# Loading one row block of the last batch in three parts: 1632 columns on all 128 partitions, 544 columns as 36 and 92 partitions

## The chip, the cores and the metric

The kernel runs on one core of a Trainium2 chip. The metric is the device time of one execution in microseconds (us), as the median of several runs. Engines are named as in the profile: PE (TensorE, matrix products and transposes), PEld (its weight loads), DVE (VectorE), ACT (ScalarE), POOL (GpSimd) and SP (SyncE). Sixteen DMA engines move data between the chip's main memory and the core's on-chip memory of 128 partitions.

## The reference

There are eight pairs of matrices of 2176 by 2176 float32 values. For each pair the trace of the product is wanted, so eight numbers in all:

```python
B, N = 8, 2176
prod = np.matmul(a, b)
traces = np.diagonal(prod, axis1=1, axis2=2).sum(axis=-1)   # shape (8,)
```

The trace needs no full product: it is the sum over all i and k of a[i, k] * b[k, i]. Each element of `a` and of `b` is used once, against the transposed partner.

## The kernel before

**Tiling.** N is 17 blocks of P = 128. The kernel speaks of 17 "rows" of `b`: row v is the block of 128 matrix rows from 128 v on, one matrix row on each partition and 2176 columns along it. For each batch the matrix `a` is loaded, transposed by the PE in 128 by 128 squares (lines 151 and 175), and copied out of PSUM by ACT and DVE into the tile `at` (lines 121 and 123). Then `b` is loaded, and `multiply_reduce` (line 128, on DVE) multiplies rows of `at` by rows of `b` and sums along the columns into one column of partial sums.

**Loads.** All loads but the first go out from POOL by `dma_start`, and convert float32 in main memory to bfloat16 in the destination. `in_order` ties each issue behind the issue before it, so POOL issues them in the order in which they are written. `fetch` (line 75) is the ordinary load: all 128 partitions, one contiguous stretch for each partition.

**The last batch** is cut finer, because nothing follows that could cover its end. `a` comes as two groups of six rows and one of five, and `b` by `fine = [4, 4, 4, 2, 1, 1, 1]` rows to a load. In this order:

- rows 0-3, 4-7 and 8-11: three loads of four rows. DVE multiplies rows 0-3, 4-7 and 8-10; row 11 goes to PE.
- rows 12 and 13: one load, all on PE.
- row 14: one load, then one DVE instruction over 2176 columns.
- row 15 (`SHARED_ROW`): one load; PE takes columns 0 to 1023 and DVE the other 1152.
- row 16: three loads by `LAST_PIECES` (line 273): columns 768-2175, then 256-767, then 0-255. DVE multiplies columns 768-1407 (640 of them), PE takes the rest.

A row on PE is 17 products of 128 by 128 (line 287) that add into the one PSUM tile `trace_ps`. Products into `unread` stand between them; nothing reads their result. At the end DVE multiplies `trace_ps` by the identity and sums it (tile `diagonal`, line 128), PE adds up the partitions (line 306), DVE adds up the columns (line 309), and SP stores the eight numbers (line 312).

**Semaphores of the loads.** The loads from POOL take eight completion semaphores in turn. A load that takes a semaphore again waits for the load that had it eight loads earlier, if nothing before has made that sure. Of the last loads, the piece of 256 columns waits in this way for the load of rows 0-3.

Of the kernel before, what the change touches and what calls it, by code (L numbers as in the profile page):

```python
# [10 lines left out]
def row_groups(p, rows):  # L11

    groups, at = [], 0
    for m in rows:
        groups.append((at, m))
        at += m * p
    return groups
# [3 lines left out]
def kernel(  # L21
# [6 lines left out]
    nc = tc.nc  # L28
    P = 128
    BATCH, N, N2 = a.shape  # L30
# [21 lines left out]

    LAST_PIECES = [(6 * P, 11 * P, N), (2 * P, 2 * P, 6 * P), (0, 0, 2 * P)]

    KEEP_BUSY = {11: 7, 13: 6, SHARED_ROW: 2}

    const = ctx.enter_context(tc.tile_pool(name="const", bufs=1))
# [7 lines left out]
    loaded = []  # L65

    def in_order():

        return tc.issue_after(loaded[-1].ins) if loaded else nullcontext()

    def fetch(t, src, start, g, m):

        rows = src[start:start + P * g * m, :].rearrange("(g p r) k -> p g (r k)", g=g, r=m)
        with in_order():
            issued = nc.gpsimd.dma_start(out=t.rearrange("p (g r) k -> p g (r k)", g=g), in_=rows)  # L75
        loaded.append(issued)
        return t

    def load(src, start, g, m):

        if g * m <= MID:
            t = middle.tile([P, MID, N], bf16, tag="middle")
        else:
            t = stage.tile([P, MOST, N], bf16, tag="stage")
        return fetch(t[:, 0:g * m, :], src, start, g, m)

    def load_first(src, start):

        words = stage.tile([P, MOST, N], bf16, tag="stage")
        plain = words.bitcast(f32).rearrange("p r k -> p (r k)")[:, :N]  # L90
        half = N // 2
        t = single.tile([P, 1, N], bf16, tag="single")
        nc.sync.dma_start(out=plain, in_=src[start:start + P, :])
        nc.scalar.copy(out=t[:, 0, :half], in_=plain[:, :half])  # L94
        nc.vector.tensor_copy(out=t[:, 0, half:], in_=plain[:, half:])  # L95
        return t
# [4 lines left out]
    def constants():  # L101
        identity32 = const.tile([P, P], f32, tag="identity32")
        make_identity(nc, identity32)
        identity16 = const.tile([P, P], bf16, tag="identity16")
        make_identity(nc, identity16)
        ones = const.tile([P, 1], f32, tag="ones")
        nc.vector.memset(ones, 1.0)
        sums = const.tile([P, (BATCH - 1) * per_batch], f32, tag="sums")
        late = const.tile([P, 2 * NT], f32, tag="late")
        diagonal = const.tile([P, P], bf16, tag="diagonal")  # L110
        result = const.tile([P, BATCH], f32, tag="result")
        tiles.update(ones=ones, sums=sums, late=late, result=result, diagonal=diagonal)
        tiles[f32], tiles[bf16] = identity32, identity16
# [12 lines left out]
    def multiply_reduce(x, y, acc, out=None):  # L126

        nc.vector.tensor_tensor_reduce(  # L128
            out=x if out is None else out, in0=x, in1=y, scale=1.0, scalar=0.0,
            op0=MUL, op1=ADD, accum_out=acc,  # L130
        )
# [54 lines left out]
    def multiply_on_pe(at, row, v, lo, hi):  # L186

        for c in range(lo, hi, P):
            pe_work.append((at[:, v, c:c + P], row[:, c:c + P]))

    def keep_pe_busy(at, v):

        x = at[:, v, :]
        pe_work.extend([(x[:, 0:P], x[:, 0:4 * P])] * KEEP_BUSY.get(v, 0))

    late = []
    ahead = None
    for bi in range(BATCH):
        last = bi == BATCH - 1
        b_groups = row_groups(P, fine if last else even)  # L200


        at = at_pool.tile([P, NT, N], bf16, tag="at")
        at_row = 0
        for g, m in last_loads if last else a_loads if bi else first_loads:
            start = at_row * P
            at_row += g * m
            if not tiles:
                a_t = load_first(a[bi], start)
                ahead = load(a[bi], start + P * m, *first_loads[1])  # L210
                with tc.issue_after(loaded[-1].ins):
                    constants()
            elif ahead is not None:
                a_t, ahead = ahead, None
            else:
                a_t = load(a[bi], start, g, m)
            for s in range(g):
                last_transpose = transpose_group(
                    at, a_t[:, s * m:(s + 1) * m, :], start + s * m * P, m, b_groups
                )  # L220


        copies_end = last_copy
        acc = tiles["late"] if last else tiles["sums"][:, bi * per_batch:(bi + 1) * per_batch]
        cols = 0

        def on_dve(v0, rows):

            nonlocal cols
            m = rows.shape[1]  # L230
            with tc.issue_after(copies_end.ins):
                multiply_reduce(
                    at[:, v0:v0 + m, :].rearrange("q v x -> q (v x)"),
                    rows.rearrange("q v x -> q (v x)"),
                    acc[:, cols:cols + 1],
                )
            cols += 1

        if not last:
            at_row = 0  # L240
            for g, m in b_loads:
                on_dve(at_row, load(b[bi], at_row * P, g, m))
                at_row += g * m
            continue

        used = MOST
        for start, m in b_groups:
            v0 = start // P
            if start < N - P:

                if used + m > MOST:
                    shared = stage.tile([P, MOST, N], bf16, tag="stage")
                    used = 0
                b_t = fetch(shared[:, used:used + m, :], b[bi], start, 1, m)
                used += m
                if v0 == SHARED_ROW:
                    row = b_t[:, 0, :]
                    multiply_on_pe(at, row, v0, 0, HALF)
                    keep_pe_busy(at, v0)
                    late.append((at[:, v0, HALF:], row[:, HALF:]))  # L260
                    continue
                mine = [s for s in range(m) if v0 + s not in PE_ROWS]
                if mine:
                    on_dve(v0 + mine[0], b_t[:, mine[0]:mine[-1] + 1, :])
                for s in range(m):
                    if s not in mine:
                        multiply_on_pe(at, b_t[:, s, :], v0 + s, 0, N)
                        keep_pe_busy(at, v0 + s)
                continue
            row = shared[:, used, :]  # L270
            for lo, mid, hi in LAST_PIECES:
                with in_order():
                    loaded.append(nc.gpsimd.dma_start(  # L273
                        out=row[:, lo:hi], in_=b[bi, start:start + P, lo:hi]
                    ))
                multiply_on_pe(at, row, v0, mid, hi)
                if mid > lo:
                    late.append((at[:, v0, lo:mid], row[:, lo:mid]))
# [5 lines left out]
    for n, (x, y) in enumerate(pe_work):  # L284
        real = y.shape[-1] == P
        with tc.issue_after(before.ins):
            before = nc.tensor.matmul(  # L287
                trace_ps if real else unread[:, 0:4, :], x, y,
                start=(n == 0 or not real), stop=(n == len(pe_work) - 1 or not real),
# [7 lines left out]
        out=result[:1, 0:done],  # L297
        in_=total[:, 0:early].rearrange("o (b n) -> o b n", n=per_batch),
        axis=mybir.AxisListType.X,
    )  # L300
    for x, y in late:
# [8 lines left out]
        out=result[:1, done:BATCH], in_=total[:, early:early + cols], axis=mybir.AxisListType.X  # L310
    )
    nc.sync.dma_start(
        out=out.rearrange("(a b) -> a b", a=1),
        in_=tiles["result"][:1, :BATCH],
# [31 lines left out]
```

## Time and profile before

| what | value |
|---|---|
| median of 3 runs | 708.98 us (708.90 to 709.16) |
| span of the profiled execution | 707.1 us |
| own time of the profiled execution | not recorded; the median is 1.88 us above the span |
| moved by DMA (as bytes written) | 152.31 MB, 215 GB/s on the mean |
| DMA packets | 7698 |
| busy share of the span | PE 28%, DVE 55%, ACT 29%, POOL 3% |
| read from main memory | 303.04 MB, 429 GB/s over the span |
| loads of the last batch's `b`, issue to landing, median | 33.1 us for each of rows 14 and 15; 33.4 us for the 256-column piece |

A busy time is the sum of an engine's instructions. The DMA line of the profile gives, for each of 40 equal slices of the span, the mean busy share of the 16 DMA engines in tenths; in a window's row the same is given as a fraction. "Issue to landing" is the time from the DMA's issue on POOL to its last completion. The times in the text are counted from the span's start.

### The profile page before, as it was taken

The page shows a single profiled execution, that of the slowest core. Times are in us where ns is not written, and L with a number is a line of the kernel's source. Part 1 is how long each engine was busy: PE and PEld are TensorE (multiplying, and loading weights), DVE is VectorE, ACT ScalarE, POOL GpSimd, SP SyncE. Part 2 cuts the span into 40 slices and gives each one's busy share as a digit, 9 for nine tenths or more (in the row PEclk, how much of TensorE's full clock was granted, in tenths as well). Part 3 has the DMA queues.
Part 4 walks back from the last instruction along what each step waited for, and adds up shares of the span by engine and source line. Part 5 has one row for each costly group of instructions (what it writes and reads, how often), then busy time and mean ns, then how long its engine had stood idle before and what let it go on. Part 6 is the DMA issues. An engine that isn't in the chain of part 4 may idle for free.

```text
span 707.1 us, 3653 instructions
## 1 busy us (share of the span) xinstructions
PE 200.8 (28%) x1569; PEld 179.8 (25%) x1569; DVE 386.8 (55%) x98; ACT 202.9 (29%) x160; POOL 24.7 (3%) x47
## 2 busy tenths in 40 slices
PE   2235003450134501344012440134301353003806
PEld 1234002440123401243012430124301343003703
DVE  0105488154881539616397163961629627395497
ACT  2327002470024700346004350044500445002910
POOL 1000000000000000000000000000000000000100
PEclk9759555695557955678556785567755677555957
DMA  9999999999999999999999999999999999999997
GB/s 236 213 217 212 225 206 214 216 224 214 224 215 213 223 213 214 216 223 218 215 217 216 215 222 213 216 223 211 221 216 216 222 214 217 216 220 213 217 211 151
DMA packets 7698, 152.31 MB, mean 215 GB/s; under 512 B 642, under 2 KB 898, under 8 KB 1282
## 3 DMA queue, kind: packets, MB, share of 16 engines
q0 software_dynamic: 7536, 150.96, 99.6%
q1 hardware_dynamic: 146, 1.11, 0.4%
q8 instruction: 12, 0.20, 0.1%
q14 instruction: 4, 0.03, 0.0%
HBM read 303.04 MB, written 0.00 MB: 429 GB/s over the span
## 4 chain that ended last, share of the span: by engine, by line
DVE 33%; another core or an unknown queue 27%; ACT 13%; PE 12%; DMA 11%; issue 3%; POOL 0%; ACTq 0%; DVEq 0%; POOLq 0%
DVE at L128 33%; ACT at L123 13%; PE ps L151 9%; DMA t<-in_a_dram 6%; DMA shared<-in_b_dram 5%; PE ps L175 2%; DVE at L121 0%; POOL shared L75 0%; PE trace_ps L287 0%; POOL shared L273 0%; POOL identity masks.py:199 0%; POOL identity masks.py:197 0%; ACTq L123 0%; DVE diagonal L128 0%
## 5 line engine op out<-in xcount | busy, mean ns | idle before, releaser
L123 ACT COPY at<-ps 128x1536 bf16<-128x1536 bf16 (+5 forms) x158 | 200.5, 1359 | 467.2 <-DVE sums L128 308.6
L128 DVE CUSTOM_DVE_ANT_0 at<-at,t 128x10880 bf16<-128x10880 bf16 (+1 forms) x14 | 272.0, 19426 | 96.3 <-DMA t<-in_b_dram 86.6
L151 PE MATMUL ps<-identity,t 128*128 128x128 f32 x833 | 147.1, 344 | 471.6 <-DMA t<-in_a_dram 378.6
L151 PEld LDWEIGHTS ps<-identity,t 128*128 128x128 f32 x833 | 131.3, 209 | 484.6 <-issue 380.3
L121 DVE COPY at<-ps 128x1536 bf16<-128x1536 bf16 (+3 forms) x52 | 83.4, 1604 | 205.8 <-PE ps L151 152.5
L175 PE MATMUL ps<-identity,t 128*128 128x128 bf16 x646 | 45.8, 227 | 11.0 <-ACT at L123 8.6
L175 PEld LDWEIGHTS <-t 128*128 128x128 bf16 x646 | 43.1, 119 | 14.7 <-issue 14.2
L128 DVE CUSTOM_DVE_ANT_0 at<-at,shared 128x8704 bf16<-128x8704 bf16 (+4 forms) x6 | 29.9, 5001 | 1.8 <-DMA shared<-in_b_dram 1.7
L75 POOL DMA_DIRECT2D t<-in_a_dram x16 | 10.1, 637 | 294.1 <-DVE sums L128 267.4
L75 POOL DMA_DIRECT2D t<-in_b_dram x14 | 8.7, 628 | 290.8 <-PE ps L175 290.5
L287 PEld LDWEIGHTS <-at 128*128 128x128 bf16 x86 | 6.8, 112 | 24.7 <-issue 23.9
L287 PE MATMUL trace_ps<-shared,at 128*128 128x128 bf16 x71 | 5.8, 241 | 21.0 <-DMA shared<-in_b_dram 20.9
L75 POOL DMA_DIRECT2D shared<-in_b_dram x6 | 3.2, 541 | 59.3 <-DVE sums L128 38.9
L287 PE MATMUL unread<-at 128*128 128x512 bf16 x15 | 5.2, 496 | 0.0
L296 DVE TENSOR_REDUCE result<-total 1x7 f32<-1x14 f32 x1 | 0.2, 159 | 7.8 <-PE total L295 7.8
L95 DVE CAST t<-words 128x1088 bf16<-128x1088 f32 x1 | 0.7, 727 | 4.9 <-DMA words<-in_a_dram 4.9
L94 ACT CAST t<-words 128x1088 bf16<-128x1088 f32 x1 | 1.1, 1099 | 3.7 <-DMA words<-in_a_dram 3.7
L273 POOL DMA_DIRECT2D shared<-in_b_dram x3 | 1.6, 552 | 1.9 <-DMA shared<-in_b_dram 1.9
L94 ACT ACT_TABLE_LOAD x1 | 1.3, 1283 | 0.7 <-PEq L330 0.7
L128 DVE DVE_READ_ACCUMULATOR2_ANT sums<- 128x1 f32 x14 | 1.2, 83 | 0.0
L128 DVE CUSTOM_DVE_ANT_0 diagonal<-identity,trace_ps 128x128 bf16<-128x128 f32 x1 | 0.3, 289 | 0.6 <-PE trace_ps L287 0.6
L128 DVE DVE_READ_ACCUMULATOR2_ANT late<- 128x1 f32 x7 | 0.6, 83 | 0.0
(12 smaller groups left out, 2.1 us busy)
## 6 DMA issues: line engine op xcount, KB each, us to landing
t<-in_a_dram POOLq DMA_DIRECT2D x8, 6528.0 KB, 55.1
t<-in_b_dram POOLq DMA_DIRECT2D x7, 6528.0 KB, 52.8
t<-in_b_dram POOLq DMA_DIRECT2D x7, 2720.0 KB, 22.1
t<-in_a_dram POOLq DMA_DIRECT2D x7, 2720.0 KB, 24.8
shared<-in_b_dram POOLq DMA_DIRECT2D x3, 2176.0 KB, 36.0
t<-in_a_dram POOLq DMA_DIRECT2D x1, 2176.0 KB, 14.7
words<-in_a_dram SPq DMA_DIRECT2D x1, 1088.0 KB, 5.0
shared<-in_b_dram POOLq DMA_DIRECT2D x1, 1088.0 KB, 30.5
```

The costliest lines, as they stand in the source:

```text
L75: issued = nc.gpsimd.dma_start(out=t.rearrange("p (g r) k -> p g (r k)", g=g), in_=rows)
L94: nc.scalar.copy(out=t[:, 0, :half], in_=plain[:, :half])
L95: nc.vector.tensor_copy(out=t[:, 0, half:], in_=plain[:, half:])
L121: last_copy = nc.vector.tensor_copy(out=dst, in_=src)
L123: nc.scalar.copy(out=dst, in_=src)
L128: nc.vector.tensor_tensor_reduce(out=x if out is None else out, in0=x, in1=y, scale=1.0, scalar=0.0, op0=MUL, op1=ADD, accum_out=acc,)
L151: nc.tensor.transpose(ps[:, n * m + r, :], words[:, r, c0:c0 + step * (P - 1) + 1:step], tiles[f32],)
L175: last_transpose = nc.tensor.transpose(ps16[:, n, r, :], a_t[:, r, c0:c0 + step * (P - 1) + 1:step], tiles[bf16],)
L273: loaded.append(nc.gpsimd.dma_start(out=row[:, lo:hi], in_=b[bi, start:start + P, lo:hi]))
L287: before = nc.tensor.matmul(trace_ps if real else unread[:, 0:4, :], x, y, start=(n == 0 or not real), stop=(n == len(pe_work) - 1 or not ...
L296: nc.vector.reduce_sum(out=result[:1, 0:done], in_=total[:, 0:early].rearrange("o (b n) -> o b n", n=per_batch), axis=mybir.AxisListType.X,)
```

## The change

Row 14 of the last batch is loaded by the new function `fetch_uneven` in place of `fetch`. It sees each matrix row of 2176 columns as two halves of 1088 and issues three loads in place of one:

- columns 272 to 1087 of both halves (1632 columns together), on all 128 partitions;
- columns 0 to 271 of both halves (544 columns together), on the first 36 partitions;
- the same 544 columns, on the other 92 partitions.

The bytes, the destination, and the work on them are as before; DVE's product over row 14 now needs all three loads.

```diff
+    UNEVEN_ROW, UNEVEN, LOW_SHARE = 14, 272, 36
...
+    def fetch_uneven(t, src, start):
+
+        halves = t[:, 0, :].rearrange("p (h k) -> p h k", h=2)
+        rows = src[start:start + P, :].rearrange("p (h k) -> p h k", h=2)
+        for p0, p1, lo, hi in [
+            (0, P, UNEVEN, N // 2), (0, LOW_SHARE, 0, UNEVEN), (LOW_SHARE, P, 0, UNEVEN)
+        ]:
+            with in_order():
+                loaded.append(nc.gpsimd.dma_start(
+                    out=halves[p0:p1, :, lo:hi], in_=rows[p0:p1, :, lo:hi]
+                ))
+        return t
...
-                b_t = fetch(shared[:, used:used + m, :], b[bi], start, 1, m)
+                if v0 == UNEVEN_ROW:
+                    b_t = fetch_uneven(shared[:, used:used + m, :], b[bi], start)
+                else:
+                    b_t = fetch(shared[:, used:used + m, :], b[bi], start, 1, m)
```

With two more loads in the list, the eight completion semaphores fall differently on the loads that follow. In the built program row 15's load now waits for the last load of `a`, the 1408-column piece for the load of rows 0-3, the 512-column piece for rows 4-7, and the 256-column piece for rows 8-11.

## The prediction

> **What bounds the kernel now.** I read the page's slices first: the DMA row is at 9 tenths in 39 of 40 slices and 7 in the last, while no compute engine is near full. Then the chain that ended last, from 640 us on: its last long link is the load of `b`.
>
> ```profile
> 668.07 35.47 DMA shared<-in_b_dram
> 703.54 0.04 issue
> 703.58 0.63 PE trace_ps L287 x6
> 704.21 0.03 issue
> ```
>
> So the end is: last load lands, PE's last products (L287), the diagonal, the sum, the store. Whatever moves the last landing moves the end one for one. Next, windows over the last microseconds. Columns: window, length, busy time and count for PE, PEld, DVE, ACT and POOL, granted PE clock, DMA share, GB/s.
>
> ```profile
> 700.00:701.00 1.00, 0.00 (x0) 0.00 (x0) 1.00 (x1) 0.00 (x0) 0.00 (x0) 1.00 1.04 192
> 701.00:702.00 1.00, 0.78 (x10) 0.64 (x10) 0.94 (x3) 0.00 (x0) 0.00 (x0) 1.00 0.91 153
> 702.00:703.00 1.00, 0.32 (x3) 0.05 (x1) 0.65 (x3) 0.00 (x0) 0.00 (x0) 1.00 0.45 71
> 703.00:704.00 1.00, 0.86 (x12) 0.66 (x11) 0.76 (x2) 0.00 (x0) 0.00 (x0) 1.00 0.15 20
> ```
>
> The reader sees all 16 DMA engines busy until 701, then a ragged end: 0.45 of them in the next-to-last and 0.15 in the last microsecond with transfers. The time is set by the latest engines, not by the mean. The sixteen completions of the 256-column load say how ragged: eight come at 701.53 to 702.38, four at 702.76 to 702.88, four at 703.68 to 703.89. Their mean is 702.58, so even a perfect levelling could bring 703.89 - 702.58 = 1.31 us.
>
> Where the three groups come from is in the queue rows:
>
> ```profile
> q0 software_dynamic: 7536, 150.96, 99.6%
> q8 instruction: 12, 0.20, 0.1%
> ```
>
> The packet records show 12 instruction packets of 16384 bytes, 0.89 to 1.00 us each. Following each engine's sequence of packets by start and duration, all run at one rate, and after an instruction packet one engine is about 0.9 us behind for good. Eight engines are never hit, four once, four twice. The records carry no engine numbers.
>
> **The change, part by part.** Packets of one size follow each other in the records at fixed distances: 4352 bytes (row 14's now) 323 ns, 2816 bytes 210 ns, 1024 bytes 79 ns, 512 bytes 41 ns; each load ends with a completion packet of 21 ns. Interpolated, an estimate from these rows: 1632 bytes (816 columns) 123.5 ns, 544 bytes (272 columns) 43.4 ns.
>
> Removed, on each engine: 8 rows x 323 + 21 = 2605 ns.
> Added, first load: 8 rows x 2 x 123.5 + 21 = 1997 ns on each engine.
> Added, the other two: how 36 or 92 partitions are shared among 16 engines no row shows; every load of the trace from POOL has 128. Bounds: as even as the row of 128 (8 pieces-of-row per engine), or packed in equal whole shares on few engines. The sizes speak for the second: 36 = 12 x 3 and 92 = 4 x 23, and 12 + 4 = 16. I take that. Twelve engines then carry 3 x 2 x 43.4 + 21 = 281 ns and a bare completion packet of 21; four carry 23 x 2 x 43.4 + 21 = 2017 ns and 21.
>
> Sums: twelve engines 1997 + 281 + 21 = 2299, against 2605: **0.31 us earlier**. Four engines 1997 + 2017 + 21 = 4035: **1.43 us later**. The end follows from which four: an engine that now ends at t ends at t + 1.43 or t - 0.31, and everything after row 14 is shared evenly, so the offsets stay to the end.
>
> The Trainium skill ("DMA: Bandwidth & Descriptors", section "Why a DMA increments its semaphore by 16 and not by 1") says that a load runs on the largest number of engines up to 16 that divides its partitions, and below 16 on consecutive engines from a cursor that moves on, which would make 12 and then the other 4; it adds an exception with partitions/16 rounded up per engine, 3 and 6 here. No run here shows either yet. By the exception twelve engines would carry 3 + 6 row pieces, three 6 and one 2: 0.22 us later on twelve. The same page's "Rules for kernel authors" speaks against the change: two transfers to disjoint partitions serialize on the same engines, so one over 128 is better. By that the sum is only the added packets, about 0.1 us later.
>
> POOL issues two more loads, at 0.54 us by the row of the single ones (533 to 558 ns): row 15's issue moves from about 667.0 to 668.1. The queue then holds the loads of rows 4 to 14, some 30 us of transfers, and hides it: nothing. The waits matter more, as POOL's queue is in order. Row 15's load waits for the last load of `a`, landed at 660.4: nothing. The 1408-column piece waits for rows 0-3 (landed 670.2), the 512 for rows 4-7 (680.5), the 256 for rows 8-11 (690.8). Behind them only those pieces are queued. Now the last issue is at 670.51; it becomes 691. The first engine reaches the 256 columns at 701.16, 10 us later: I take nothing. If that cover were gone, every microsecond beyond it would be paid in full.
>
> DVE's product over row 14 (2.43 us, start 698.71) needs three semaphores in place of one, and the latest of them lands with the latest engine: 698.58 now, 698.27 if the late engines gain. The 640-column product after it has waited 0.35 us for its own load and ends at 703.76, before PE's 704.21: DVE stays off the path. PE's instructions are the same, so instruction packets should fall as now.
>
> **The cases.** The sums stand against the span of 707.1; the median of the runs is 1.88 us above it, and I carry differences over to 708.98.
>
> 1. The four loaded engines are among the eight early ones (701.53 to 702.38). They end at 702.96 to 703.81; the late ones at 703.89 - 0.31 = 703.58. For seven of the eight the gain is 0.26 to 0.31, for the latest 0.08: **708.7** (708.6 to 709.0). For it speaks the sizing: 1.43 + 0.31 = 1.74 of shift is about what lies between the early group and the late one.
> 2. One of the four has had one instruction packet (702.76 to 702.88): end at 704.19 to 704.31, 0.30 to 0.42 later: 709.3 to 709.4.
> 3. The rival on the other side: one of the four has had two instruction packets. 703.68 to 703.89 plus 1.43 is 705.11 to 705.32, 1.22 to 1.43 later: 710.2 to 710.4. It decides as soon as a single late engine is in the set. Against it: only four of sixteen are late. For it: four drawn freely miss all late ones in 495 of 1820 ways. Were the 544-byte packets dearer than interpolated (bound: 79 ns, the 1024-byte row), the 46 of them add up to 1.6 us more; I stay near 43, the 512-byte row being nearest, but a few ns take this case past 710.4.
> 4. The change does not do what it says: the shares stay even. Then 1997 + 8 x 2 x 43.4 + 42 = 2733 against 2605, 0.13 later, or 0.22 with nine pieces on the late ones: 709.1 to 709.2.
> 5. The last load comes late: if POOL cannot write it while DVE multiplies. After 690.8 DVE runs its third product until 697.93, then others until 702.57. No row shows an issue under such a product. Freed at 697.9, it costs about nothing; freed at 702.57 and with the 3.7 us that the very first load took from issue to first packet, 706.3 against 701.16 to 703.6, some 2.7 to 5 later: 711.7 and more.
>
> **How the numbers follow.** Chances: case 1 0.46, case 2 0.11, case 3 0.32, case 4 0.06, case 5 0.05. Two in a thousand, 1.42 us, is about what a measurement of this kernel can tell from no change. Faster by more than that is out of reach of every sum (the ceiling is 1.31): 0.03 for what I have not seen. Slower by more: most of case 3, as it ends on the bound and small costs push it over, and case 5: 0.28. Within: 0.69. The predicted time is that of case 1, 708.7; the range goes from its best with 0.15 of spread to the upper end of case 3, 708.5 to 710.5.
>
> **What would show it.** Right: packets of 1632 and 544 bytes at 123 and 43 ns; the load of 36 partitions ends early on twelve engines and that of 92 keeps four busy for 2.0 us; the 256-column completions end at about 703.6, with four early ones moved up by 1.4. Wrong: a last group beyond 705 (case 3), around 704.3 (case 2), shares of 3 and 6 rows (case 4), or DMA engines idle before the last piece (case 5). What would overturn the working altogether is an end that is not the last landing.

## The result, and the profile after

The changed kernel took 710.48 us (median of 20 runs, 709.31 to 710.74) against 708.95 us before (20 runs, 708.80 to 709.22): ratio 1.0017, 95% interval [1.0011, 1.0024]. It is slower, by 0.2%. The median hides two groups. With the 11 runs of a later repetition, 8 of 31 runs lie at 709.31 to 709.55 us (median 709.35) and 23 at 710.32 to 710.96 us (median 710.53), none between. The kernel before shows one group. The profiled execution of the changed kernel took 709.44 us (span 707.7) and belongs to the lower group.

The chain that ended last, after, from where the last loads are issued (start, length, what):

```profile
680.83 23.30 DMA shared<-in_b_dram
704.13 0.04 issue
704.17 0.63 PE trace_ps L305 x6
704.80 0.03 issue
```

The end still hangs on a landing at the end of the load stream, and it comes 0.59 us later than before (PE's last products start at 704.17 in place of 703.58). The prediction took it for the very last landing; it is the one before that. In the kernel before the chain's load starts at 668.07, with the second of the three pieces of row 16 and not with the third (POOL's issues, start and length):

```profile
667.55 1.09 POOL L273 DMA_DIRECT2D shared<-in_b_dram  x2
670.51 0.53 POOL L273 DMA_DIRECT2D shared<-in_b_dram  x1 [1.88 <-DMA shared<-in_b_dram]
```

So the chain ends on the 512-column load: its last completion is at 703.54 before and at 704.13 after. The 256 columns land 0.34 us later in both, while PE still multiplies the 512 columns. Both landings moved by the same 0.59 us, so the reading changes no number.

The link of the kernel after is cut at 680.83 because an issue now waits there for an earlier load; that wait is not what the end waits for, as shown further down. The windows over the end, columns as before:

```profile
701.00:702.00 1.00, 0.11 (x2) 0.11 (x2) 0.95 (x3) 0.00 (x0) 0.00 (x0) 1.00 0.93 162
702.00:703.00 1.00, 0.93 (x10) 0.53 (x9) 1.00 (x1) 0.00 (x0) 0.00 (x0) 1.00 0.60 106
703.00:704.00 1.00, 0.45 (x6) 0.37 (x6) 0.71 (x3) 0.00 (x0) 0.00 (x0) 1.00 0.38 55
704.00:705.00 1.00, 0.66 (x7) 0.36 (x5) 0.43 (x3) 0.00 (x0) 0.00 (x0) 1.00 0.05 6
```

The same row from 704 on in the kernel before:

```profile
704.00:705.00 1.00, 0.39 (x4) 0.11 (x3) 0.37 (x3) 0.00 (x0) 0.00 (x0) 1.00 0.00 0
```

The ragged end is longer: DMA shares of 0.60, 0.38 and 0.05 from 702 on, where it was 0.45, 0.15 and 0.00. The same bytes end less level than before. The queue row and the packets say what else was added (queue, packets, MB, share of the engines):

```profile
q0 software_dynamic: 8528, 150.97, 99.7%
DMA packets 8690, 152.31 MB, mean 215 GB/s; under 512 B 1250, under 2 KB 2018, under 8 KB 2274
```

992 packets more on queue 0. In the packet records 128 of 4352 bytes are gone; 256 of 1632 and 256 of 544 have come, and 32 completion packets for two more loads: that makes 416. The other 576 have 4 bytes, last 9 ns and follow each other every 6 ns. 576 is 12 x 46 + 4 x 6: for every packet that a load gives to a busy engine, each engine that has no rows of that load gets one bare packet, a packet of 4 bytes without data of the load. This also fixes the shares, for no other equal shares of 36 and 92 rows give this count: 12 engines with 3 rows, 4 with 23.

The completions confirm it engine by engine. In what follows the early, middle and late groups are the eight, four and four engines that instruction packets had visited never, once and twice. Row 14's 128-partition load completes at 695.74 to 696.36 (eight engines), 697.09 to 697.13 (four) and 697.88 to 698.05 (four, the late ones). The load of 92 completes about 0.6 us after that on twelve engines, so the four late ones stand at 698.48 to 698.73; on the loaded four it is 2.05 to 2.09 us after: at 698.18 on one of the early group, and at 699.18 to 699.23 on three of the middle group. Those three then are the last of the 256-column load, at 704.45 to 704.47; the late ones are at 703.75 to 703.92. This is case 2 of the prediction. The case of the other 23 runs the experiments have to show.

Case 5, a late last issue, is refuted by POOL's timeline and DVE's product beside it (start, length, engine, line, operation, idle time before and what ended it):

```profile
680.83 0.53 POOL L291 DMA_DIRECT2D shared<-in_b_dram  x1 [9.72 <-DMA shared<-in_b_dram]
691.18 0.53 POOL L291 DMA_DIRECT2D shared<-in_b_dram  x1 [9.82 <-DMA shared<-in_b_dram]
691.05 6.96 DVE L143 CUSTOM_DVE_ANT_0 at<-at,shared 128x6528 bf16<-128x6528 bf16 x1 [0.67 <-DMA shared<-in_b_dram]
```

The 512- and 256-column loads are issued at 680.83 and 691.18, as the wait for rows 4-7 and 8-11 demands. Both take the usual 0.53 us although DVE multiplies all the while (the first lies under its product of 9.21 us from 672.02 on), and the 16 engines stay busy (share 0.93 to 1.08) up to 702. The wait costs nothing.

### The profile page after: what moved, and what is told of

It is laid out like the page before. It is cut to its first block, busy times and chain, and to the rows that moved or that the text cites. A ratio compares the mean times of both kernels' runs of the same rounds, so it can differ in the third digit from the quotient of the medians.

```text
span 707.7 us, 3656 instructions
## 1 busy us (share of the span) xinstructions
PE 202.8 (29%) x1569; PEld 181.4 (26%) x1569; DVE 386.8 (55%) x98; ACT 203.0 (29%) x160; POOL 26.7 (4%) x49
## 4 chain that ended last, share of the span: by engine, by line
DVE 39%; another core or an unknown queue 20%; DMA 15%; ACT 13%; PE 9%; issue 3%; POOL 0%; ACTq 0%; DVEq 0%; POOLq 0%
DVE at L143 38%; ACT at L138 13%; DMA shared<-in_b_dram 8%; PE ps L166 7%; DMA t<-in_a_dram 6%; PE ps L190 2%; PE trace_ps L305 0%; POOL shared L77 0%; POOL identity masks.py:199 0%; POOL identity masks.py:197 0%; ACTq L138 0%; DVE diagonal L143 0%; PE total L324 0%; DVE sums L143 0%
## 5 line engine op out<-in xcount | busy, mean ns | idle before, releaser
L77 POOL DMA_DIRECT2D shared<-in_b_dram x5 | 2.7, 548 | 59.2 <-DVE sums L143 38.7
L89 POOL DMA_DIRECT2D shared<-in_b_dram x3 | 2.5, 832 | 0.0
L291 POOL DMA_DIRECT2D shared<-in_b_dram x3 | 1.6, 538 | 20.5 <-DMA shared<-in_b_dram 20.5
```

The lines of the kernel that those rows point to most:

```text
L89: loaded.append(nc.gpsimd.dma_start(out=halves[p0:p1, :, lo:hi], in_=rows[p0:p1, :, lo:hi]))
L291: loaded.append(nc.gpsimd.dma_start(out=row[:, lo:hi], in_=b[bi, start:start + P, lo:hi]))
```

## The experiments

Theory A is that the place of the heavy load decides: four engines carry 23 rows, and the time depends on whether instruction packets have put these four behind. Theory B is that three loads cost more than one wherever the rows go. Rival C is that the loads themselves begin at another engine from run to run.

**The change once more.**

> The changed kernel once more, unaltered. Theory A (placement): the load of 92 partitions gives 23 rows to each of four engines, and the time depends on whether these four are engines that instruction packets have put behind, which differs from run to run; so the times fall into the same two groups, about 709.4 and 710.5 us, and a profile of the slow group must show heavily loaded engines among those that were already last before row 14, with the last landing near 705.3 us (703.89 of before plus about 1.45). Theory B (count): three loads cost more than one wherever the rows go (more packets, more completions, later issues); then a profile of the slow group shows all sixteen engines later by the same amount.

Measured: 710.58 us against 708.95, ratio 1.0021 [1.0012, 1.0030], and the two groups again (2 low, 9 high). The profiled execution was in the lower group once more (709.34 us), with the same picture: heavy load on three engines of the middle group and one early one. So the groups are real, but no profile of this kernel fell in the upper one.

**Same loads, even shares.**

```diff
-            (0, P, UNEVEN, N // 2), (0, LOW_SHARE, 0, UNEVEN), (LOW_SHARE, P, 0, UNEVEN)
+            (0, P, UNEVEN, N // 2), (0, 64, 0, UNEVEN), (64, P, 0, UNEVEN)
```

> Same three loads with the same columns, but the 544 columns as 64 and 64 partitions in place of 36 and 92. Theory A: 64 shares evenly over 16 engines, 4 rows each, so every engine does 1997 + 2 x (8 x 43.4 + 21) = 2733 ns against 2605: 0.13 us later, 709.1 us, and one group of times. Theory B: as many loads, waits and issues as the change, so 709.4 to 710.5 us as there.

Measured: 709.09 us against 708.95 (1.0002 [0.9993, 1.0011]), one group, 0.14 us above. The sum said 0.13; the interval takes in no difference too, and in the profile the last completion is 0.17 us later than before (704.05 against 703.88). There are no bare packets. As many loads, semaphores, waits and issues as the change, and nearly none of its cost: theory B falls.

**The 92 partitions first.**

```diff
-            (0, P, UNEVEN, N // 2), (0, LOW_SHARE, 0, UNEVEN), (LOW_SHARE, P, 0, UNEVEN)
+            (0, P, UNEVEN, N // 2), (LOW_SHARE, P, 0, UNEVEN), (0, LOW_SHARE, 0, UNEVEN)
```

> The load of 92 partitions before that of 36. Theory A with a cursor that moves over the engines: the 92 partitions go to another four engines. If these are among the eight that no instruction packet hits, 708.9 us (twelve engines 0.03 earlier, four early ones 1.46 later but still not last) and one group of times; if they are engines that instruction packets hit, two groups as in the change, 709.4 and 710.5. Theory B, or a cursor that always begins at the same engine so that nothing moves: 710.5 as the change.

Measured: 708.94 us against 708.95 (1.0000 [0.9991, 1.0009]), one group of 11. The same two loads in the other order cost nothing: the order decides which engines carry the rows. In its completions the four that end the 92 partitions about 2.04 us after the main load are all of the early group. This is case 1 of the prediction in the flesh, and its gain is not there. The interval, about 0.6 us to each side, is wider than the 0.25 us that case 1 promised, so the profile has to say it: the last completion is at 704.13, against 703.88 before, and PE's last products start 0.24 us later, not earlier:

```profile
703.82 0.63 PE trace_ps L305 x6
```

**A heavy load of 116, in one piece per row.**

```diff
+        for p0, p1, lo, hi in [
+            (0, P, 368, N), (0, 4, 0, 368), (4, 120, 0, 368), (120, P, 0, 368)
+        ]:
```

> Row 14 as 1808 columns on 128 partitions and 368 columns in one piece per row on 4, then 116, then 8 partitions: 116 = 4 x 29 is the heavy load, and the 4 in front should move it on by four engines from where a heavy load issued first goes. By the packet rows: four engines 2158 + 29 x 58 + 84 = 3924 ns, 1.32 us later than with one load; the other twelve 2158 + 58 + 29 x 6 + 84 = 2474 ns, 0.13 us earlier. Theory A: 708.8 us if the four are engines that no instruction packet hits, 709.3 and 710.3 in two groups if they are hit. Theory B: four loads in place of three, later still than the change, 711 us.

Measured: 709.06 us against 708.95 (1.0001 [0.9992, 1.0010]), one group. The expectation failed on its premise: the completions of the load of 116 follow those before it by about 0.2 to 0.4 us on all engines, so no engine carried 29 rows. There are 32 bare packets (704 packets of 4 bytes on queue 0, less 16 completions for each of 42 loads) where 29 rows on each of four engines need 348. 32 is what fills up the other engines if no engine gets more than 1, 8 and 1 rows of the loads of 4, 116 and 8: 12 + 12 + 8. A load with one contiguous piece per row is dealt out nearly evenly over the 16.

**A heavy load of 116 in two pieces per row, at two other places.**

```diff
-    UNEVEN_ROW, UNEVEN, LOW_SHARE = 14, 272, 36
+    UNEVEN_ROW, UNEVEN, LOW_SHARE = 14, 184, 36
...
+            (0, P, UNEVEN, N // 2), (0, 4, 0, UNEVEN), (4, 120, 0, UNEVEN), (120, P, 0, UNEVEN)
```

> Strips of 184 columns of both halves as loads of 4, 116 and 8 partitions, each row still in two pieces (the load in one piece per row shared its rows evenly, so it placed nothing). If a load of two pieces per row goes to the largest number of engines up to 16 that divides its partitions, one after another round the engines, 4 + 4 + 8 fill the 16 and the heavy load (116 = 4 x 29) sits on the four next to those of the kernel with the 92 first. Twelve engines: 16 x 136.9 + 21 for the main load, 58 bare 4-byte packets at 6 ns, 369, and 116 for the small loads: 2.70 us against 2.61, 0.09 later. The four: 2211 + 58 x 31 + 21 + 66 = 4.10 us, 1.49 later. Theory A: 709.0 us and one group if these four are free of instruction packets, two groups at 709.4 and 710.5 if not. Rival C (the two groups of the change come from the loads themselves, which begin at another engine from run to run): two groups here too, and in every kernel with a heavy load.

Measured: 710.32 us against 709.02 (1.0015 [1.0006, 1.0024]), two groups: 4 runs at 709.09 to 709.39, 7 at 710.21 to 710.58. This profiled execution was in the upper group (710.40 us). Its windows at the end:

```profile
703.00:704.00 1.00, 1.00 (x9) 0.72 (x7) 1.00 (x2) 0.00 (x0) 0.00 (x0) 0.50 0.25 41
704.00:705.00 1.00, 1.00 (x9) 0.68 (x8) 0.73 (x3) 0.00 (x0) 0.00 (x0) 0.50 0.14 20
```

The DMA share of 0.14 in the last full microsecond is two engines of sixteen. In the completions they are two of the four last ones of the main load (698.02 to 698.35) that then also took the heavy load: they finish it at 699.84 and 699.99 and the 256 columns at 705.16 and 705.29, while the two last ones without it are done at 703.94 and 704.11. This is case 3, seen in a profile of another kernel.

The other place, with loads of 8, 116 and 4:

> The same with loads of 8, 116 and 4 partitions: the heavy load sits four engines further on, next below the four of the change. Same sums: 0.09 us later on twelve engines, 1.49 on four. Theory A: if instruction packets visit one half of the sixteen engines, and the heavy load of the change lies in that half, these four are in it as well: two groups, about 709.4 and 710.5 us. If they are free: 709.0 and one group. Rival C: two groups whatever the place.

Measured: 710.29 us against 709.02 (1.0016 [1.0007, 1.0025]), 2 runs low, 9 high. One engine ends after all others here, at 705.22. So of four places for the heavy load, one shows no delayed engine in any of its 11 runs, and three do. My guess that the eight hit engines form one half is wrong: they lie in all three other places. Rival C is left without support, since the 92-first kernel, with its heavy load, has one group.

**What makes the two groups.** If instruction packets go round eight engines, 12 of them reach four engines twice, and which four depends on where the turn begins. With 16 every one of the eight has two. So 512 small products on PE, 64 behind each batch's transposes, were added to both kernels:

```diff
+        for _ in range(64):
+            with tc.issue_after(last_transpose.ins):
+                last_transpose = nc.tensor.matmul(
+                    trace_ps[0:1, 0:1], tiles[bf16][:, 0:1], tiles[bf16][:, 0:1],
+                    start=True, stop=True,
+                )
```

> The kernel before with 512 products of 128 x 1 by 128 x 1 added on PE, 64 behind each batch's transposes, into a place that nothing reads: 1024 more PE instructions, so 16 instruction packets of 16384 bytes in place of 12. They are the base of the next kernel. Theory A: eight engines get two packets each; the last landing stays where it is, 708.95 us to within 0.2, and the completions of the last load fall into two groups of eight instead of 8, 4 and 4. If the packets had nothing to do with the lag, the groups 8, 4, 4 stay.

Measured: 709.10 us against 709.02 (1.0002 [0.9993, 1.0011]). The queue row shows the 16 packets:

```profile
q8 instruction: 16, 0.26, 0.1%
```

The completions of the last load fall into two groups of eight, 701.25 to 702.36 and 703.43 to 704.17, where they were 8, 4 and 4. The lag is the instruction packets' doing.

> The same 512 products added to the changed kernel. Theory A: with 16 instruction packets every one of the eight engines has two of them in every run, however the turn begins, so the heavily loaded engines among them are always among the last ones: all runs near 710.5 us, the group at 709.4 is gone, and the profiled run too is near 710.5. Rival C: the two groups stay, about three runs in ten at 709.4.

Measured: 710.65 us against 709.02 (1.0024 [1.0015, 1.0034]), and all 10 runs at 710.47 to 710.71. The lower group is gone, and rival C, under which it should have stayed, with it. The groups come from how the visits of the instruction packets fall on the loaded engines. The windows of this profile:

```profile
703.00:704.00 1.00, 0.92 (x10) 0.53 (x9) 1.00 (x1) 0.00 (x0) 0.00 (x0) 1.00 0.41 69
704.00:705.00 1.00, 0.46 (x5) 0.45 (x5) 0.71 (x3) 0.00 (x0) 0.00 (x0) 0.58 0.21 32
705.00:706.00 1.00, 1.00 (x10) 0.71 (x7) 0.36 (x2) 0.00 (x0) 0.00 (x0) 0.50 0.04 5
```

0.21 of 16 engines after 704 is three engines: the three of the heavy load's four that instruction packets visit, now all among the last. Their completions of the last load are 705.31 to 705.50, the other late ones' 703.42 to 703.96.

The lengths of the instruction packets show the turn itself. In the kernel before they are, in order, 893, 893, 948, 945, 936, 974, 975 and 962 ns, and then begin again. All twelve profiles run through this same round, to 2 ns but for one longer packet near 586 us in some. Four begin at its first length (both profiles of the change are among them), one at its third, three at its fifth and four at its seventh. So the round has eight places and does begin elsewhere from one execution to another. If each length stands for one engine, both profiles of the lower group visited the first four of the round twice, and the three loaded engines are among the other four. Were the four beginnings equally frequent, all three would be spared in one run of four, an estimate from these counts; measured are 8 of 31.

**The price of the bare packets.** The 92 first, and four strips of 136 columns in place of two of 272:

```diff
-        halves = t[:, 0, :].rearrange("p (h k) -> p h k", h=2)
+        four = t[:, 0, :].rearrange("p (h k) -> p h k", h=4)
...
+            (0, P, 136, 544), (LOW_SHARE, P, 0, 136), (0, LOW_SHARE, 0, 136)
```

> The 92 partitions first, where no instruction packet falls, and the 544 columns as four strips of 136 in place of two of 272: the heavy load is 92 packets of 272 bytes on each of its four engines. If the engines without rows of a load get one bare 4-byte packet of 6 ns for every packet of the busy ones (46 in the change), they now get 92: twelve engines 8 x 4 x 64 + 21 for the main load, 92 x 6 + 21 and 12 x 24 + 21, 2.95 us against 2.61, 0.35 later, 709.3 us; the four 1.7 to 1.8 later, so not after the others. Rival: the bare packets cost nothing, as my prediction had it by leaving them out; then twelve engines are 0.2 us earlier and the four, about level with the last, set 708.9 to 709.0 us.

Measured: 709.30 us against 708.94 (1.0006 [0.9997, 1.0015]), 0.36 above; the interval alone takes in no difference, so the records carry this reading. They hold 1152 bare packets, and the engines with none of the 92 rows end that load about 0.6 us after the main one (92 x 6 + 21 = 573 ns), against about 0.3 with two strips. Bare packets are paid for at 6 ns each. Part of the 0.36 in the time may be PE's clock, which was at 0.50 at the end of this profile: PE's last product ends 0.51 us after the last completion (704.39), where it was 0.33 us in the kernel before.

**The split of the change in one piece per row.**

```diff
+        for p0, p1, lo, hi in [
+            (0, P, 544, N), (0, LOW_SHARE, 0, 544), (LOW_SHARE, P, 0, 544)
+        ]:
```

> The same split into 36 and 92 partitions, but the 544 columns in one piece per row. If then the rows are dealt out evenly, 36 as 3 each on twelve engines and 92 as 6 each on fifteen and 2 on the last, twelve engines carry 1952 + 9 x 84 + 63 = 2771 ns, 0.17 us later, three are 0.07 and one 0.35 us earlier: 709.1 us and one group of times, or down to 708.9 when the late engines are the relieved ones. If the number of partitions alone decided and four engines carried 23 rows of 84 ns, they would be 1952 + 1932 + 63 = 3947, 1.34 us later: two groups up to 710.3 us.

Measured: 709.06 us against 708.94 (1.0001 [0.9992, 1.0010]), one group. There are 16 bare packets (672 of 4 bytes, less 16 for each of 41 loads), what a deal of 3 rows on twelve engines, and of 6 on fifteen and 2 on one, leaves to fill up: 4 x 3 + 4. The numbers 36 and 92 alone do nothing. They placed rows unevenly only where a row was cut into two or four pieces.

No version tried is faster than the kernel before by more than its interval.

## Why the prediction was wrong

**The step that failed: which four.** I put the four loaded engines into the early group, on the ground that the sizing fitted (1.43 + 0.31 = 1.74 us of shift). That reads an intention out of a size. Three of the four are engines that instruction packets visit. Even in the lower group, where each of the three has had one packet, they end last, at 704.45 to 704.47, and not at the 703.6 or so of case 1. I also took the answer to be one and the same for every run. It is not: in 8 of 31 runs these engines have had one packet each, which is case 2, in 23 it fits case 3, at which I put 0.32.

**A term that was mis-sized: the twelve engines' gain.** I gave them "a bare completion packet of 21" for the load of 92, in which they have no rows. They get 46 bare packets too: 281 + 21 + 46 x 6 = 578 ns after the main load, and the records show 0.6 us. So 1997 + 578 = 2575 stands against 2605, a gain of 0.03 us and not 0.31. The first of the late group confirms it: it takes 2.59 us for the three loads of row 14 in the change (695.89 to 698.48), 2.58 us with the 92 first, and 2.61 us for the one load before (695.76 to 698.37). Case 1 was therefore wrong even where it held: with the 92 first it gave 708.94, not 708.7.

**What held.** The end hangs on the last landings, if not on the very last. The shares are 12 x 3 and 4 x 23. 1632 and 544 bytes follow at 123 and 43 ns, and the four loaded engines were late by about what the sum said (2.05 to 2.09 us after the main load, 2.04 summed). Case 2 at 709.3 to 709.4 was measured at 709.35. Case 4 at 709.1 is the even split, 709.09. Case 3 at 710.2 to 710.4 came out at 710.53: in the upper-group profiles of the loads of 4, 116 and 8 and of the 16 instruction packets the last landing is 1.41 and 1.62 us later than before, and PE's last product ends 0.51 us behind it in place of 0.33, at a lower clock (last section). The loads of 8, 116 and 4 kept the full clock; there the last landing is 1.34 us later and the span 1.33 us longer. The waits, the later issues and DVE cost nothing, although the three issues of row 14 took 0.65 to 1.14 us each, and not 0.54, so that row 15's began at 668.98 and not at 668.1. The median lies just inside the range, but the forecast was a gain.

Of the Trainium skill ("DMA: Bandwidth & Descriptors", section "Why a DMA increments its semaphore by 16 and not by 1") both branches showed: the largest divisor up to 16 for loads of two pieces per row (bare-packet count 12 x 46 + 4 x 6), the deal over all 16 for one piece per row (32 and 16 bare packets). The row of the same page's "Rules for kernel authors" that advises against two transfers to disjoint partition halves meets its own case only in the even split, which came out 0.14 us above, inside its interval.

**What stays open:** why the turn of the instruction packets begins where it does in a run; the upper group of the change itself, which no profile caught; and why the number of pieces per row selects the way of sharing.

## What to carry to other kernels

Where the end hangs on the last landings of a stream that keeps all DMA engines busy, read the sixteen completions of the last loads: what lies between their mean and the last one is all that rebalancing can win (1.31 us here), and what put engines behind may move from run to run. Before rows are placed on chosen engines, find out what else those engines carry; the same two loads cost 1.5 us at the median in one order and nothing in the other. If times fall into two groups, vary the suspected cause until one group must vanish: 1024 added instructions did that here.

## What the runs showed of the hardware that was not expected

- An engine without rows of a load can still work for it: 46 bare 4-byte packets, 6 ns apart, for a load whose busy engines have 46 packets. Over twelve engines that ate 0.28 of 0.31 us.
- The shape of a row decides the sharing: 36 and 92 partitions with two pieces per row went to 12 and 4 engines, with one piece per row nearly evenly to all (16 bare packets in place of 576).
- Twelve instruction packets of 16384 bytes, 0.1% of the engines' time, set the shape of the whole kernel's end: about 0.9 us for each visit, kept to the end.
- A later end can meet a slower PE. In the profiles of the kernel before and of the change the granted clock is 1.00 to the last products. In the profile of the changed kernel with 16 instruction packets it fell to 0.58 and 0.50 after 704, and PE's last twelve products took 1.45 us in place of 1.25. The chain then ends with these twelve, behind the 1408-column load, and no longer with six behind the 512 columns (its chain's line stands below). The loads of 4, 116 and 8 and the four strips show 0.50 there too.

```profile
704.54 1.47 PE trace_ps L312 x12
```
